# Pairs of projections in one two-bank PSUM tile, in the first halves of a hybrid trunk step

## The chip, the cores and the metric

One core of one Trainium2 chip runs the kernel. The metric is the device time of one execution in microseconds. The engines are PE (TensorE, the matmuls), ACT (ScalarE), DVE (VectorE), POOL (GpSimd) and SP (SyncE, which issues the DMAs). Matmuls write to PSUM, which has eight banks of 2 KB per partition; 512 float32 columns fill one bank. All engines take their instructions in a fixed order that is set when the program is built; they wait for each other through semaphores.

## What is computed

Two layers over 1024 prompt tokens and 8 sample tokens. Each layer projects its input by one wide matrix, sends the parts through three branches (attention in a window of 128, a gated linear recurrence, a Mamba-2 SSD), gates each of them, projects the joined result back and normalises:

```python
def mixer_layer(x, pos, att_cache, lru_conv0, lru_h0, ssd_conv0, ssd_h0, p):
    proj = jnp.einsum('bld,de->ble', x, p['w_in'])
    q, k, v, g_att, x_lru, g_lru, z_ssd, xbc, dt_raw = jnp.split(proj, SPLIT_POINTS, axis=-1)
    q, k = partial_rope(q, pos), partial_rope(k, pos)
    att = swa_prompt(q, k, v, p['att_sinks'])          # swa_sample for the sample tokens
    br_a = att * jax.nn.silu(g_att)
    xl, lru_conv1 = causal_conv(x_lru, lru_conv0, p['lru_conv_w'], p['lru_conv_b'])
    hl, lru_h1 = rglru(xl, lru_h0, ...)
    br_b = hl * jax.nn.silu(g_lru)
    xbc_c = jax.nn.silu(causal_conv(xbc, ssd_conv0, ...))
    dt = jax.nn.softplus(dt_raw + p['ssd_dt_bias'])
    y, ssd_h1 = ssd_scan(xs, dt, a_head, b_ssm, c_ssm, ssd_h0)
    br_c = rms_norm((y + p['ssd_d'] * xs) * jax.nn.silu(z_ssd))
    out = jnp.einsum('ble,ed->bld', concat(br_a, br_b, br_c), p['w_out'])
    return layer_norm(DEEPNORM_ALPHA * x + out, p['ln_g'], p['ln_b'])
```

## The kernel before

The channels lie on the partitions and the tokens along the free dimension. The program walks four stages, layer 0 first half, layer 0 second half, layer 1 first half, layer 1 second half. A first half has W = HALF = 512 token columns, a second half 520 (512 and the 8 samples). In each stage 38 projections of 128 output channels run over the input (`project`, called for K, V, Q0 to Q3, the attention gates GA0 to GA3, the eight SSD blocks of each group, here s00 to s07 and s10 to s17, the recurrence's inputs XL0 to XL5 and its gates GL0 to GL5). `ssd_steps` adds a projection of 24 channels for the step sizes, called "steps" here. Then `out_proj` computes eight blocks of 128 channels, four times over, each time over a quarter of the joined branches.

Numbers are split into a high and a low part. So each product of 128x128 weights takes three matmuls (`mac3`): weights high by input high (L270), high by input low (L271), low by high (L272). A projection has 8 such products: 24 matmuls of 512 columns in a first half, in one bank; 48 of 260 columns in a second half, in two banks. A block of `out_proj` has 12 matmuls of 512 columns in a first half. The weights come in by DMA and are split by ACT (L225) and POOL (L226), two projections ahead.

The PSUM pool `ipp` holds two tiles of two banks, with the tag ip, and every call of `ip_tile` takes the next of them. So the projection that is called as number n waits until the result of number n-2 has been read out, its evacuation. In a first half the second bank of each of the two tiles is not used. Four more banks (`mmp`, tag mm) serve all other matmuls. The evacuation of an SSD or XL block is the pair of ACT instructions at the head of `conv` (L321, L322). That of a gate is ACT's tanh and DVE's product in `gate_silu` (L314, L315). K and Q take one ACT instruction (L716), V one (L762), the steps one (L469). A block of `out_proj` takes a DVE addition (L986).

Between projections, `pump` lets the generators of the attention, the SSD and the recurrence go on: `spawn` hands them over, and each call of `pump` counts down their delays. So the small matmuls of the branches stand between the large ones. The framework then orders the instructions of each engine for good: it simulates the schedule with estimated durations, takes the order in which instructions become ready, and inserts the semaphore waits. For each tile it keeps who last wrote and read it, and the next tile in the same place waits for its last reader.

Of the kernel before, what the change touches and what calls it, by code (L numbers as in the profile page):

```python
# [11 lines left out]
F32 = mybir.dt.float32  # L12
# [5 lines left out]
P = 128  # L18
# [4 lines left out]
HALF = 512  # L23
# [27 lines left out]
def tile_trunk(ctx, tc, outs, x_t, cache_k, cache_v, st_lru_conv, st_ssd_conv, st_ssd_h, w_in, w_dt, w_out,  # L51
# [13 lines left out]
    ipp = ctx.enter_context(tc.tile_pool(name="ipp", bufs=2, space=bass.MemoryType.PSUM))  # L65
    mmp = ctx.enter_context(tc.tile_pool(name="mmp", bufs=4, space=bass.MemoryType.PSUM))

    def ip_tile():
        return ipp.tile([P, 2, 512], F32, tag="ip", name="ip")

    def mm_tile():
        return mmp.tile([P, 512], F32, tag="mm", name="mm")
# [7 lines left out]
    def wtile(shape, tag, bufs=1, dt=F32):  # L80
        return wk.tile(shape, dt, tag=tag, name=tag, bufs=bufs)
# [128 lines left out]
    def pump():  # L210
        for t in list(tasks):
            t[0] -= 1
            if t[0] <= 0:
                try:
                    t[0] = next(t[2])
                except StopIteration:
                    tasks.remove(t)
# [38 lines left out]
    def weights(key):  # L256

        load_weights()
        k, w = loaded.pop(0)
        assert k == key  # L260
        return w
# [7 lines left out]
    def mac3(out, wh, wl, xh, xl, first, last):  # L269
        PE.matmul(out, wh, xh, start=first, stop=False)  # L270
        PE.matmul(out, wh, xl, start=False, stop=False)  # L271
        PE.matmul(out, wl, xh, start=False, stop=last)  # L272
# [7 lines left out]

    def project(l, x, W, block):
        w = weights((l, block))
        ps = ip_tile()
        for c, (k0, k1) in (((0, (0, 4)), (0, (4, 8))) if W == HALF else ((0, (0, 8)), (1, (0, 8)))):
            pump()
            out, cs = pc(ps, W, c)
            for k in range(k0, k1):
                mac3(out, w.h[:, k, :], w.l[:, k, :], x[0][k // 4][:, k % 4, cs], x[1][k // 4][:, k % 4, cs],
                     k == 0, k == 7)
        return ps  # L290

    def chunks(W):

        return [slice(0, W)] if W == HALF else [slice(0, W // 2), slice(W // 2, W)]

    def pc(ps, W, c):

        if W == HALF:
            return ps[:, 0, :], slice(0, W)
        n = W // 2  # L300
        return ps[:, c, :n], slice(c * n, (c + 1) * n)
# [6 lines left out]
    def sv(ap, W):  # L308
        return ap.rearrange("p (c n) -> p c n", c=2)
# [147 lines left out]
    def ssd_steps(st, l, half, x):  # L457

        W = HALF + NS * half
        ps = ip_tile()  # L460
        pump()
        for c in range(len(chunks(W))):
            out, cs = pc(ps, W, c)
            for k in range(8):
                for i in range(2):
                    PE.matmul(out[:24], wdt[:, l, k, :], x[i][k // 4][:, k % 4, cs], start=k + i == 0,
                              stop=k + i == 8)
        dtr = wtile([24, WMAX], "ev", NE)
        S.activation(sv(dtr[:, :W], W), pv(ps, W, 24), AF.Copy)  # L469

        def rest():
            pt = mm_tile()
            for b in range(4):
                PE.matmul(pt[:, b * 12:b * 12 + 12], dtr[:, b * P:(b + 1) * P], sel, start=True, stop=True)
            if half:
                PE.matmul(pt[:NS, 48:60], dtr[:, HALF:W], sel, start=True, stop=True)
            nd = 48 + 12 * half
            dv = wtile([P, 60], "dv")
            if half:
                G.memset(dv[:, 48:60], 0.0)  # L480
            V.tensor_tensor(dv[:, :48].rearrange("p (b e) -> p b e", b=4),
                            pt[:, :48].rearrange("p (b e) -> p b e", b=4),
                            dtb_bc[:, l, None, :].to_broadcast([P, 4, 12]), ALU.add)
            if half:
                V.tensor_tensor(dv[:NS, 48:60], pt[:NS, 48:60], dtb_bc[:NS, l, :], ALU.add)
            dt = st["dt"] = wtile([P, 60], "dt")
            dsc = wtile([P, 4, 60], "dsc")
            softplus(dt[:, :nd], dv[:, :nd], [dsc[:, i, :nd] for i in range(4)], nd)
            da = st["da"] = wtile([P, 60], "da")
            V.tensor_tensor(da[:, :nd].rearrange("p (b e) -> p b e", e=12),  # L490
                            dt[:, :nd].rearrange("p (b e) -> p b e", e=12),
                            a_bc[:, l, None, :].to_broadcast([P, nd // 12, 12]), ALU.mult)
            if half:

                sdt = wtile([NS, 2, 12], "eda")
                V.tensor_copy(sdt[:, 0, :], dt[:NS, 48:60])
                S.activation(sdt[:, 1, :], da[:NS, 48:60], AF.Exp)
                sdd = dp.tile([2, 12, NS], F32, tag="sdd", name="sdd")
                for e in range(2):
                    dma(sdd[e].rearrange("k b -> b k"), sdt.rearrange("b q (t e) -> b (q t) e", e=2)[:, :, e])  # L500
                dcols = st["dcols"] = wtile([P, 2, 6, NS], "dcols")
                for e in range(2):
                    dma(dcols[64 * e:64 * e + 64].rearrange("p a b c -> p (a b c)"),
                        bview(sdd, e * 96, [[0, 64], [1, 96]]))
            yield 7
            pc = mm_tile()
            PE.matmul(pc[:, 0:48], tri, da[:, :48], start=True, stop=True)
            PE.matmul(pc[:, 64:112], ones, da[:, :48], start=True, stop=True)

            nacs = st["nacs"] = wtile([P, 48], "acs")  # L510
            V.tensor_scalar(nacs, pc[:, 0:48], -1.0, None, op0=ALU.mult)
            cd = st["cd"] = wtile([P, 48], "cd")
            S.activation(cd, pc[:, 64:112], AF.Exp)
            dd = st["dd"] = wtile([P, 48], "dd")
            V.tensor_tensor(dd, pc[:, 64:112], nacs, ALU.add)
            S.activation(dd, dd, AF.Exp)
            V.tensor_tensor(dd, dd, dt[:, :48], ALU.mult)
            yield 1
            pa = mm_tile()
            PE.transpose(pa[:48, :P], nacs, ident)  # L520
            acsT = wtile([48, P], "q", NC)
            V.tensor_copy(acsT, pa[:48, :P])
            acsd = st["acsd"] = dp.tile([48, P], F32, tag="acsd", name="acsd")
            dma(acsd, acsT)
            st["steps"] = True

        spawn("ssd", rest())
# [424 lines left out]
    def out_proj(l, half, mixd, load_next, first):  # L952
        W = HALF + NS * half
        n = W // 2
        r = [u_tile() for _ in range(2)]
        for i in range(2):
            dma(r[i][:, :, :W], xd[l, half][512 * i:512 * i + 512, :W].rearrange("(k p) w -> p k w", p=P))
        cur = first
        for gi, (g, _) in enumerate(GROUPS):
            mh, ml = cur  # L960
            if gi < 3:
                drain(*GROUPS[gi + 1][1])
                cur = load_mix(half, mixd, GROUPS[gi + 1][0])
            if gi == 2:
                load_next()


            split_c = l == LAYERS - 1 and half == 1 and gi == 3
            for part in ((slice(HALF // 2, W), slice(0, HALF // 2)) if split_c else (None,)):
                for op in range(4):  # L970
                    w = weights((l, g, op))
                    for oo in range(2):
                        pump()
                        o = 2 * op + oo
                        ps = ip_tile()
                        if part:
                            products = [(ps[:, 0, :part.stop - part.start], part)]
                        else:
                            products = [pc(ps, W, c) for c in range(len(chunks(W)))]
                        for out, cs in products:  # L980
                            for k in range(4):
                                mac3(out, w.h[:, k, oo * P:oo * P + P], w.l[:, k, oo * P:oo * P + P],
                                     mh[:, k, cs], ml[:, k, cs], k == 0, k == 3)
                        ro, po = r[o // 4][:, o % 4, :W], pv(ps, W)
                        ro, po = (ro[:, part], products[0][0]) if part else (sv(ro, W), po)
                        V.scalar_tensor_tensor(ro, ro, ALPHA if gi == 0 else 1.0, po, op0=ALU.mult, op1=ALU.add)  # L986
                if part and part.start:
                    spawn("norm", norm_last(half, r, (2, 3, 4)))
        return r
# [266 lines left out]
```

## Time and profile before

| | us |
|---|---|
| median of 3 runs (lowest, highest) | 1747.94 (1747.93, 1750.72) |
| the profiled execution, its own time | 1744.72 |
| its span in the trace | 1743.0 |
| PE busy in the span | 1601.8 (92%) |
| DVE, ACT, POOL busy | 1177.5, 960.3, 915.4 |
| mean granted clock of PE | 0.963 of full speed |

The profiled execution took 1.7 us more than its span, and 3.2 us less than the median. The stages lie as follows in the trace: projections of layer 0's first half to 304 us, its out_proj to 412, the second half to 866, layer 1's first half to 1178, its out_proj to 1292, the second half to 1743. In the timeline a row is the start, the duration, the engine, the line, the operation, its output and inputs with their shapes, and in brackets the idle time before it with what ended that.

### The profile page before, as it was taken

What the parts mean: (1) busy time and instruction counts of PE and PEld (TensorE: products, weight loads), DVE (VectorE), ACT (ScalarE), POOL (GpSimd) and SP (SyncE); (2) the same over time, 40 slices, a digit from 0 to 9 for tenths busy, and PEclk for the clock granted to TensorE, in tenths of its full rate; (3) what the DMA queues carried; (4) which work ended last, traced back from release to release, by engine and by line L of the source; (5) the groups of instructions that cost most, each with busy time, mean ns of one, the idle gap of its engine ahead of it and who ended that gap; (6) DMA issues with size and microseconds to landing.
All of it is one profiled execution on the core that took longest, in us unless ns stands there. A gap on an engine that the chain in (4) does not pass through costs nothing. (4 is left out here: it accounts for less than half of the span.)

```text
span 1743.0 us, 29885 instructions
## 1 busy us (share of the span) xinstructions
PE 1601.8 (92%) x10696; PEld 1353.7 (78%) x10696; DVE 1177.5 (68%) x2118; ACT 960.3 (55%) x2066; POOL 915.4 (53%) x866
## 2 busy tenths in 40 slices
PE   8999998899889998889998999988998998988996
PEld 6777765578889887779966777656798997977896
DVE  5756578835955877876488565679336659788835
ACT  5655567723455646675155555666345646566724
POOL 4544655445444667644444445553445547786344
PEclk9999999999899989899999999999999999989999
DMA  6322334732232545455323223347433234453733
GB/s 228 98 87 84 100 97 144 238 114 88 82 110 84 157 122 149 128 200 184 104 68 129 77 88 102 92 135 238 148 117 101 84 111 145 122 149 108 238 121 123
DMA packets 147294, 222.00 MB, mean 127 GB/s; under 512 B 17077, under 2 KB 56961, under 8 KB 147097
## 3 DMA queue, kind: packets, MB, share of 16 engines
q1 hardware_dynamic: 144840, 215.90, 39.4%
q10 hardware_dynamic: 2304, 4.20, 0.7%
q8 instruction: 84, 1.38, 0.3%
q14 instruction: 66, 0.53, 0.1%
HBM read 184.04 MB, written 35.43 MB: 126 GB/s over the span
## 5 line engine op out<-in xcount | busy, mean ns | idle before, releaser
L226 POOL TENSOR_TENSOR wl<-wraw,wh 128x512 fp32r<-128x512 f32 x440 | 619.7, 1426 | 609.4 <-ACT wh L225 557.5
L270 PE MATMUL ip<-u,wh 128*128 128x260 f32 (+3 forms) x2592 | 861.9, 333 | 62.2 <-DVE u L986 20.9
L272 PE MATMUL ip<-u,wl 128*128 128x260 f32 (+3 forms) x2592 | 846.5, 327 | 7.3 <-POOL wl L226 7.2
L271 PE MATMUL ip<-u,wh 128*128 128x260 f32 (+3 forms) x2592 | 847.0, 327 | 0.0
L270 PEld LDWEIGHTS ip<-u,wh 128*128 128x128 f32 x2592 | 500.3, 193 | 130.1 <-issue 21.0
L272 PEld LDWEIGHTS ip<-u,wl 128*128 128x128 f32 x2592 | 499.8, 193 | 52.7 <-POOL wl L226 9.1
L271 PEld LDWEIGHTS ip<-u,wh 128*128 128x128 f32 x2592 | 500.7, 193 | 44.8 <-issue 8.5
L225 ACT ACTIVATE wh<-wraw 128x512 fp32r<-128x512 f32 x440 | 256.5, 622 | 314.4 <-PE ip L271 140.9
L986 DVE SCALAR_TENSOR_TENSOR u<-u,ip 128x512 f32<-128x512 f32 (+3 forms) x136 | 89.0, 655 | 150.6 <-PE ip L272 150.6
L329 DVE SCALAR_TENSOR_TENSOR u<-ev,ssd_p,u 128x512 f32<-128x512 f32 x120 | 117.6, 980 | 27.4 <-ACT u L322 22.1
L827 ACT ACTIVATE sp<-sp,mx 128x257 f32<-128x257 f32 (+1 forms) x128 | 62.4, 490 | 75.6 <-DVE mx L823 75.6
L329 DVE SCALAR_TENSOR_TENSOR u<-ev,lru_p,u 128x512 f32<-128x512 f32 x72 | 79.0, 1098 | 19.7 <-ACT u L322 19.4
L614 ACT ACTIVATE acr<-acr,acs 128x128 f32<-128x128 f32 x192 | 63.0, 393 | 44.4 <-POOL acr L611 30.8
L424 PE MATMUL mm<-u,gw 96*32 96x260 f32 (+1 forms) x576 | 62.0, 495 | 23.6 <-DVE hst L633 11.2
L608 POOL TENSOR_TENSOR cq<-cq,u 128x384 f32<-128x384 f32 x56 | 63.5, 1136 | 34.9 <-ACT cq L607 22.0
L233 DVE TENSOR_TENSOR u<-u 128x512 fp32r<-128x512 f32 (+1 forms) x88 | 71.3, 846 | 12.8 <-ACT u L232 12.7
L616 DVE TENSOR_TENSOR acr<-acr,q 128x384 f32<-128x384 f32 x64 | 45.7, 737 | 35.6 <-ACT q L602 27.6
L823 DVE CUSTOM_DVE_ANT_0 sp<-mm,amask,sp 128x256 f32<-128x256 f32 (+1 forms) x128 | 54.7, 463 | 20.2 <-PE mm L820 20.0
L607 ACT ACTIVATE cq<-acr 128x384 f32<-128x384 f32 x56 | 29.1, 522 | 70.7 <-DMA acr<-acsd 66.4
L232 ACT ACTIVATE u<-u 128x512 fp32r<-128x512 f32 (+1 forms) x88 | 51.7, 626 | 26.1 <-DVE sd L564 12.0
L315 DVE SCALAR_TENSOR_TENSOR u<-ev,ip 128x512 f32<-128x512 f32 (+1 forms) x48 | 33.0, 687 | 40.8 <-ACT ev L314 33.6
L424 PEld LDWEIGHTS mm<-u,gw 96*32 96x32 f32 x576 | 17.0, 114 | 50.0 <-issue 19.8
(281 smaller groups left out, 2216.2 us busy)
## 6 DMA issues: line engine op xcount, KB each, us to landing
wraw<-in_w_in_dram SPq DMA_DIRECT2D x304, 256.0 KB
wraw<-in_w_out_dram SPq DMA_DIRECT2D x136, 256.0 KB
acr<-acsd SPq DMA_DIRECT2D x64, 192.0 KB
u<-mixd SPq DMA_DIRECT2D x32, 260.0 KB
u<-mixd SPq DMA_DIRECT2D x32, 256.0 KB
mixd<-u SPq DMA_DIRECT2D x24, 260.0 KB
h<-in_st_ssd_h_dram SPq DMA_DIRECT2D x32, 192.0 KB
mixd<-u SPq DMA_DIRECT2D x24, 256.0 KB
```

The lines of the kernel that those rows point to most:

```text
L225: S.activation(dh, src, AF.Copy)
L226: G.tensor_tensor(dl, src, dh.bitcast(F32), ALU.subtract)
L233: V.tensor_tensor(dl, raw, dh.bitcast(F32), ALU.subtract)
L270: PE.matmul(out, wh, xh, start=first, stop=False)
L271: PE.matmul(out, wh, xl, start=False, stop=False)
L272: PE.matmul(out, wl, xh, start=False, stop=last)
L329: V.scalar_tensor_tensor(out[:, :HALF], raw[:, t:t + HALF], prm[:, wo + t:wo + t + 1], out[:, :HALF], op0=ALU.mult, op1=ALU.add)
L424: PE.matmul(ps[c0:c1, :n], gw[:, gi, k, b0:b0 + c1 - c0], xc[:96, k, cs], start=True, stop=True, skip_group_check=True)
L608: G.tensor_tensor(cq[i], cq[i], zc[:, None, 3, cs].to_broadcast([P, 3, P]), ALU.mult)
L614: S.activation(acr[i][:, e, :], acr[i][:, e, :], AF.Exp, scale=-1.0, bias=nacs[:, eb + 3 * i + e:eb + 3 * i + e + 1])
L827: S.activation(s[:, kv, :nk + 1], s[:, kv, :nk + 1], AF.Exp, scale=-1.0, bias=mx[:, kv:kv + 1], accum_out=den[:, kv:kv + 1])
L986: V.scalar_tensor_tensor(ro, ro, ALPHA if gi == 0 else 1.0, po, op0=ALU.mult, op1=ALU.add)
```

## The change

`ip_tile` is told the width. In a first half, one call takes a new tile of two banks and gives out its bank 0; the call after it gives out bank 1 of the same tile. Any other width takes a whole tile as before. The pairs go by order of call: (K, V), (steps, Q0), (GA0, s00), (s01, Q1), (GA1, s02), (s03, Q2), (GA2, s04), (s05, Q3), (GA3, s06), (s07, s10), and so on through (s17, XL0), (XL1, XL2), (GL0, GL1), (GL2, XL3), (XL4, XL5), (GL3, GL4), (GL5, first block of out_proj), and the blocks of out_proj two by two.

```diff
-    def ip_tile():
-        return ipp.tile([P, 2, 512], F32, tag="ip", name="ip")
+    second = []
+
+    def ip_tile(W):
+
+        if W == HALF and second:
+            return second.pop()
+        second.clear()
+        t = ipp.tile([P, 2, 512], F32, tag="ip", name="ip")
+        if W == HALF:
+            second.append(t[:, 1:2, :])
+            t = t[:, 0:1, :]
+        return t
...
     def project(l, x, W, block):
         w = weights((l, block))
-        ps = ip_tile()
+        ps = ip_tile(W)
...
     def ssd_steps(st, l, half, x):
         W = HALF + NS * half
-        ps = ip_tile()
+        ps = ip_tile(W)
...
                         o = 2 * op + oo
-                        ps = ip_tile()
+                        ps = ip_tile(W)
```

All lines below L79 move down by ten, so that L270 becomes L280. The order of the instructions moves in the first halves alone. A row of the order is the line, the operation, and the tiles that it writes and reads, with their numbers.

The first place is on PE in layer 0, behind GA0. Before, s00 (tile ip_448) follows GA0 (tile ip_375) in the order of the calls:

```order
L271 MATMUL ip_375<-u_117,wh_311 128x512
L272 MATMUL ip_375<-u_115,wl_312 128x512
L270 MATMUL ip_375<-u_115,wh_311 128x512
L271 MATMUL ip_375<-u_117,wh_311 128x512
L272 MATMUL ip_375<-u_115,wl_312 128x512
L270 MATMUL ip_448<-u_114,wh_365 128x512
L271 MATMUL ip_448<-u_116,wh_365 128x512
```

After, the tile ip_373 holds GA0 in bank 0 and s00 (weights wh_363) in bank 1, and ip_498 begins with s01 (weights wh_436):

```order
L280 MATMUL ip_498<-u_114,wh_436 128x512
L281 MATMUL ip_498<-u_116,wh_436 128x512
L282 MATMUL ip_498<-u_114,wl_437 128x512
L280 MATMUL ip_498<-u_115,wh_436 128x512
L281 MATMUL ip_498<-u_117,wh_436 128x512
L280 MATMUL ip_373<-u_114,wh_363 128x512
L281 MATMUL ip_373<-u_116,wh_363 128x512
L282 MATMUL ip_373<-u_114,wl_364 128x512
```

The block s01, which is called behind s00, has moved ahead of it, and s00 starts in the middle of s01, 14 of whose matmuls stand between GA0's last one and s00's first one.

The second place is on PE where the recurrence's projections begin. Before, XL1 (tile ip_2174), whose place is that of s17, follows XL0 (ip_2130) and a small matmul:

```order
L271 MATMUL ip_2130<-u_117,wh_2019 128x512
L272 MATMUL ip_2130<-u_115,wl_2020 128x512
L270 MATMUL ip_2130<-u_115,wh_2019 128x512
L271 MATMUL ip_2130<-u_117,wh_2019 128x512
L272 MATMUL ip_2130<-u_115,wl_2020 128x512
L619 MATMUL mm_2175<-sd_2075,q_2077 128x384
L270 MATMUL ip_2174<-u_114,wh_2120 128x512
L271 MATMUL ip_2174<-u_116,wh_2120 128x512
L272 MATMUL ip_2174<-u_114,wl_2121 128x512
```

After, s16 is bank 1 of ip_1866, and XL1 takes bank 0 of ip_2160, which is that tile's place:

```order
L280 MATMUL ip_1866<-u_115,wh_1856 128x512
L281 MATMUL ip_1866<-u_117,wh_1856 128x512
L282 MATMUL ip_1866<-u_115,wl_1857 128x512
L634 MATMUL mm_2019<-acr_1914,sd_1923 64x128 x2
L634 MATMUL mm_2019<-cq_1933,hst0_112 64x128
L634 MATMUL mm_2019<-cq_1936,hst0_112 64x128
L634 MATMUL mm_2019<-acr_1914,sd_1923 64x128
L634 MATMUL mm_2019<-acr_1915,sd_1923 64x128
L634 MATMUL mm_2019<-cq_1936,hst0_112 64x128 x2
L634 MATMUL mm_2019<-acr_1915,sd_1923 64x128 x2
L280 MATMUL ip_2160<-u_114,wh_2107 128x512
L281 MATMUL ip_2160<-u_116,wh_2107 128x512
```

The last matmuls of s16 now stand directly ahead of XL1, with ten small matmuls of the SSD between them, where a whole projection stood.

## Rows read from the trace of the kernel before

**Rows 1.** The page: PE's busy time; and POOL's weight split as a group.

```profile
PE 1601.8 (92%) x10696; PEld 1353.7 (78%) x10696; DVE 1177.5 (68%) x2118; ACT 960.3 (55%) x2066; POOL 915.4 (53%) x866
L226 POOL TENSOR_TENSOR wl<-wraw,wh 128x512 fp32r<-128x512 f32 x440 | 619.7, 1426 | 609.4 <-ACT wh L225 557.5
```

**Rows 2.** Windows by stage: length, PE, PEld, DVE, ACT, POOL, clock, DMA, GB/s.

```profile
6.00:304.00 298.00, 285.22 (x1474) 213.89 (x1475) 202.07 (x393) 174.30 (x395) 158.77 (x152) 0.98 0.36 117
304.00:412.00 108.00, 98.28 (x418) 74.67 (x417) 65.52 (x81) 46.77 (x75) 45.66 (x33) 0.97 0.51 166
412.00:866.00 454.00, 414.36 (x3413) 384.29 (x3412) 323.20 (x594) 247.04 (x533) 251.75 (x238) 0.95 0.42 129
866.00:1178.00 312.00, 290.58 (x1497) 218.69 (x1496) 217.70 (x364) 176.46 (x390) 155.76 (x149) 0.97 0.32 100
1178.00:1292.00 114.00, 106.90 (x515) 84.68 (x514) 60.91 (x83) 52.20 (x87) 49.38 (x37) 0.99 0.52 167
1292.00:1743.00 451.00, 406.47 (x3389) 377.50 (x3388) 307.12 (x605) 258.63 (x574) 251.08 (x238) 0.95 0.42 131
```

**Rows 3.** PE's waits, 6 to 304, then 866 to 1178: total, times, longest.

```profile
PE ip L270 <- DVE ga L315: 4.4, 2, 4.1
PE ip L270 <- DVE u L315: 2.0, 1, 2.0
...
PE ip L270 <- DVE u L315: 5.7, 1, 5.7
PE ip L270 <- DVE ga L315: 5.6, 3, 2.8
PE ip L270 <- ACT u L322: 3.5, 2, 3.3
```

**Rows 4.** Timeline, layer 0: GA0's last matmul, s00's, GA0's evacuation, the next start.

```profile
36.84 0.40 PE L272 MATMUL ip<-u,wl 128*128 128x512 f32 x1
...
43.62 0.40 PE L272 MATMUL ip<-u,wl 128*128 128x512 f32 x1
...
47.34 0.67 DVE L315 SCALAR_TENSOR_TENSOR ga<-ev,ip 128x512 f32<-128x512 f32 x1
...
48.07 0.71 PE L270 MATMUL ip<-u,wh 128*128 128x512 f32 x1 [4.06 <-DVE ga L315]
```

**Rows 5.** Timeline, layer 0: the end of s11, its evacuation, and small matmuls.

```profile
152.78 0.40 PE L272 MATMUL ip<-u,wl 128*128 128x512 f32 x1
153.02 0.40 PE L270 MATMUL ip<-u,wh 128*128 128x512 f32 x1
...
154.09 0.58 ACT L321 ACTIVATE ev<-ip 128x512 f32<-128x512 f32 x1
...
154.57 0.77 ACT L322 ACTIVATE u<-ip,ssd_p 128x512 f32<-128x512 f32 x1
...
154.50 0.66 PE L848 MATMUL mm<-sp,vtok 128*64 128x128 f32 x8
```

**Rows 6.** Timeline, layer 0: the last matmul of s16 and its evacuation.

```profile
193.03 0.39 PE L272 MATMUL ip<-u,wl 128*128 128x512 f32 x1
...
195.89 0.69 DVE L315 SCALAR_TENSOR_TENSOR u<-ev,ip 128x512 f32<-128x512 f32 x1 [3.03 <-ACT ev L314]
```

**Rows 7.** Timeline, layer 1: the slowest evacuation, of Q1, and GA0's.

```profile
895.34 0.40 PE L272 MATMUL ip<-u,wl 128*128 128x512 f32 x1
...
907.09 0.68 DVE L315 SCALAR_TENSOR_TENSOR ga<-ev,ip 128x512 f32<-128x512 f32 x1
...
919.77 0.39 PE L272 MATMUL ip<-u,wl 128*128 128x512 f32 x1
...
935.17 0.58 ACT L716 ACTIVATE ev<-ip 128x512 f32<-128x512 f32 x1
```

**Rows 8.** Windows behind two idle stretches of PE, columns as in rows 2.

```profile
48.00:52.00 4.00, 3.93 (x10) 3.12 (x11) 3.73 (x10) 2.94 (x6) 2.55 (x2) 0.57 0.06 21
924.00:929.00 5.00, 3.26 (x8) 2.62 (x9) 5.00 (x11) 3.49 (x9) 2.13 (x3) 0.66 0.65 238
```

## The prediction

> **What bounds the kernel now.** I read the page first. PE is busy 92% of the span and no other engine over 68% [rows 1], so PE carries the time, and a change is worth what it adds to PE's idle time or takes from it. The windows by stage then say where the change can act. The order of the built program has the same PE rows in the second halves before and after (454 and 451 us, the third and the sixth row of [rows 2]), so these 905 us should stay. The first halves hold 298 + 108 + 312 + 114 = 832 us, of which PE is busy 285.2 + 98.3 + 290.6 + 106.9 = 781.0 us, so it idles 51 us [rows 2]. All that the change can save lies in these 51 us; what it can cost has no such limit.
>
> The waits of PE then show how much of that comes from places in PSUM. In the two stretches with projections PE stood still at L270 for an evacuation 4.4 + 2.0 us in layer 0 and 5.7 + 5.6 + 3.5 us in layer 1: 21.2 us in nine waits [rows 3]. The other idle time belongs to weights and to the branches' own chains, which the change leaves as they are.
>
> The timeline shows why so few starts wait. Start n needs the evacuation of n-2, and the whole of n-1 lies between: 24 matmuls at 0.24 us from one to the next (the first two of [rows 5]), 5.8 us, with small matmuls besides. I call the PE work between the last matmul of the awaited projection and the start that waits for it the cover. An evacuation, counted from that last matmul to the end of the last reading instruction, took 2.2 us where ACT was at hand (153.18 to 155.34, [rows 5]), 3.2 us for s16 [rows 6], 10.8 us for GA0 (37.24 to 48.01, [rows 4]) and 15.6 us at most (920.16 to 935.75, [rows 7]). Over the 78 of the two stretches I work out a mean of 5.0 and a median of 4.1 us from the timeline, of which these are the quick end and the slow one. A cover of 5.8 us and more hides most of them.
>
> **The change part by part.** The matmuls, evacuations, weight splits and DMAs keep their number and size. What changes is which start waits for what, and so the order on PE.
>
> First, the waits. The change gives four banks, and by its words four projections have a place. In the built program they don't quite. The waits there go by tiles: the second projection of a pair, in bank 1, waits for the count that the evacuation of bank 0 of its own tile sets; the first projection of a tile waits for both evacuations of the tile two before it. So there are still two chains. Only who waits for whom has changed: the second of a pair waits for its partner, which is called directly ahead of it, and the first of the next pair waits for the second one of the pair before the last.
>
> The order answers to that. PE no longer does 0, 1, 2, 3, but 0, 2, 1, 4, 3: it puts a projection of the other tile between two partners where it can. Of the 74 starts of projections and steps in the two stretches that I can compare, 3 had under 4.4 us of PE work as cover before; in the order after, 31 have. Those 31 have 2.0 us in the median; the other 43 have 4.9 to 15.7 us. The two places quoted with the change show it. XL1 comes ten small matmuls behind s16, whose evacuation it needs; eight small ones take 0.66 us [rows 5], so the cover is about 0.8 us against an evacuation of 3.2 us [rows 6]: 2.4 us of wait, where a whole projection hid it before. And s00 has 14 matmuls of s01, 3.4 us, between GA0 and itself, while GA0's evacuation took 10.8 us. Before, 6.8 us of s00's matmuls lay there and PE still idled 4.06 us [rows 4]; half the cover gone makes this wait some 3.4 us longer.
>
> The sum over all starts: where the evacuation is longer than the cover, the rest is a wait. If each evacuation took as long as before, this gives 42 us in the order before and 94 us in the order after. The rough check is 31 starts x (5.0 - 2.0) = 93 us. Now 42 is twice the 21.2 us that PE really waited, since a wait that has held PE up once holds up what comes after it as well. I take the same half for the 52 us more: +26 us. Three of the entries in the opening of layer 1 hang on one and the same chain on DVE (GA0 and Q1 of [rows 7]), and the wait is paid once: -6. Idle PE has a price behind it: after the idle 4.06 us at 44 us the granted clock was 0.57 for 4 us [rows 4, 8], that is half of full speed for most of it, and it was 0.66 for 5 us around the idle 3.3 us at 922 [rows 3, 8]. The first is (1 - 0.57) x 4 = 1.7 us. Two more such stretches: +3. Last, part of the longer wait is taken from waits that PE has anyway in the branches' chains, about 30 of the 51 us; I take -3 for that. Net: +26 - 6 + 3 - 3 = +20 us.
>
> The bounds. If each evacuation ran at its quickest (2.2 us, [rows 5]) whenever PE waits for it, the waits after would come to 11.5 us, against 21.2 now: -10 us. If all 94 us were paid, +73 us. I stand nearer to the half, because it is what the same sum gave in the order before.
>
> Second, out_proj (108 and 114 us, [rows 2]). Its blocks are paired too, and PE swaps them in the same way (1, 0, 2, 3, 5, 4). Each start still has one block of 12 matmuls, 2.9 us, between itself and the block whose addition it awaits: nothing. The other end would be some tenths for each of 64 blocks, up to 10 us, and is inside the range.
>
> Third, the weights. A projection that is moved ahead needs its weights earlier, and POOL's split takes 1.43 us for a half [rows 1], behind ACT's. The weights are still two projections ahead and the swapped one still comes a whole projection after the one before it, 5.8 us: nothing. Were that cover gone, each would cost two splits, 2.9 us. The opening K, V loses the other tile as cover too: V now waits for K's one ACT instruction, about half a microsecond.
>
> A rule that speaks against this reading: a matmul may write one bank while another engine reads a different one. The Trainium skill says so in "PSUM — Partial Sum Buffer", section "Summary: rules for kernel authors", which wants semaphores by bank. By that rule nothing on the chip asks a second projection to wait for its partner, and the waits would vanish as in the second rival below; the built program waits all the same, and no row here can show what the chip would do without.
>
> **The rivals.** *Evacuations catch up* (not slower). While PE stands still it gives ACT and DVE nothing new, and they are busy 58% and 68% of the first stretch [rows 2]; so each awaited evacuation may come near its 2.2 us. It decides where the evacuation outlasts its cover by less than 21.2 / 31 = 0.7 us at each of the 31 short starts. For it: the order was chosen for short waits. Against it: s16, a plain gate, took 3.2 us with 3.03 us of DVE idle, so ACT came late [rows 6], and ACT splits weights and serves the softmax in between. It gives 1744.7 - 10 + 3.2 = 1738 us.
>
> *The change does what it says* (faster): four projections have a place, no start of the first halves waits, and the 21.2 us go, or 1727 us by the median. Against it stand the counts that the second of each pair waits for.
>
> *No difference*: the waits on evacuations only move other idle time, since the chain of the SSD and the recurrence sets the end of each stretch: 1748 us. Against it, PE idles only 12.8 of the 298 us and 21.4 of the 312 us [rows 2], so there is little to be absorbed in.
>
> *The full price*: waits put the evacuations of the next projections no earlier, each start pays its own, +73 us: 1821 us. It decides if ACT and DVE have as long a queue when PE idles as when it doesn't.
>
> **How the numbers follow.** The profiled execution took 1744.7 us, 3.2 below the median. 1744.7 + 20 + 3.2 = 1768 us. The chances: my forecast and its neighbours, slower by some 5 to 55 us, 0.65; the full price 0.10; evacuations catch up 0.14; the change does what it says 0.02; no difference 0.09. A measurement of this kernel can tell about 0.2%, 3.5 us, from no change. So faster 0.16, the same 0.09, slower 0.75. The range for 8 in 10 reaches from just under the catch-up rival, 1736, to 1800, which leaves out the full price, the second rival and the tail of the first. The cases slower than before alone would span 1753 to 1800.
>
> **What would show it.** The waits of PE at L280 on DVE L325 and on ACT L332 and L726 in the first halves' projections should come to some 40 us instead of 21, in many waits of 1 to 3 us. The two stretches of projections should be longer by some 8 to 12 us each, the out_proj stretches by under 2 us, and the second halves unchanged. XL1 should wait for DVE L325 for about 2 us, and s00 of layer 0 for 7 us. I am wrong if these stretches are no longer than before, if the evacuations behind the short starts take 2.2 us, or if the second halves move.

## The result, and the profile after

The changed kernel took 1755.62 us in the median of 11 runs, against 1747.94 us (11 runs) for the kernel before. The ratio is 1.0051, with a 95% interval from 1.0033 to 1.0069: slower by 8.9 us, between 5.8 and 12.1. The forecast was 20 us more than before. The sign held. The size was more than twice what was measured, and the waits that were to show the mechanism moved the other way, as the list of waits below shows.

The page after the change, first PE's busy time, as in [rows 1], and then the windows by stage, as in [rows 2] (length, busy time of PE, PEld, DVE, ACT and POOL, granted clock, DMA share, GB/s):

```profile
PE 1603.3 (91%) x10696; PEld 1352.0 (77%) x10696; DVE 1167.5 (67%) x2118; ACT 960.5 (55%) x2066; POOL 906.3 (52%) x866
```

```profile
6.00:322.00 316.00, 293.83 (x1507) 216.57 (x1507) 202.96 (x399) 177.04 (x400) 157.41 (x154) 0.98 0.35 115
322.00:421.40 99.40, 93.45 (x383) 73.67 (x384) 59.86 (x75) 42.99 (x69) 42.45 (x31) 0.97 0.51 164
421.40:874.00 452.60, 413.73 (x3416) 382.72 (x3416) 324.27 (x594) 246.91 (x533) 252.00 (x238) 0.95 0.42 130
874.00:1186.00 312.00, 291.80 (x1507) 217.65 (x1505) 210.53 (x364) 177.64 (x390) 153.90 (x151) 0.97 0.31 101
1186.00:1288.00 102.00, 95.07 (x411) 74.22 (x412) 57.66 (x80) 47.04 (x75) 42.39 (x31) 0.98 0.53 178
1288.00:1753.90 465.90, 415.45 (x3479) 387.15 (x3477) 311.25 (x607) 263.84 (x587) 255.12 (x242) 0.95 0.41 128
```

The second half of layer 0 is about as long as before (452.6 against 454 us). That of layer 1 took 466.1 us (1287.8 to 1753.9) against 462.0 (1281 to 1743), with the same matmuls in the same order; so of the 10.9 us between the two profiles 4.1 lie there, outside the stages that the change touches. In layer 0 the projections and out_proj together take 415.4 us, against 406 of [rows 2]: 9.4 more. In layer 1, from the first projection to the first matmul of the second half, they took 413.8 us (874 to 1287.8), against 415.0 by the same marks before (866 to 1281). So the first halves together went from 821.0 to 829.2 us. PE is busy 770.0 and 774.0 us in these stretches: half of the 8.2 us that the first halves grew by is idle time, the other half is time in which the same matmuls took longer. How the loss lies between the stages should not be read too closely, since the same stage differed by up to 3 us between the profiles of the kernel before and of one with the same order on PE (e2 below).

PE's waits after (line, what ended them, total, times, longest), of layer 0's first half (6 to 421.4 us), then of layer 1's (874 to 1287.8), as in [rows 3] but with out_proj:

```profile
PE ip L280 <- ACT wh L235: 11.7, 4, 6.5
PE ip L280 <- DVE u L996: 5.4, 2, 2.7
PE ip L282 <- POOL wl L236: 4.3, 4, 2.7
PE ip L280 <- ACT ev L726: 3.7, 2, 3.3
PE ip L280 <- DVE u L325: 2.8, 3, 1.7
...
PE ip L280 <- ACT wh L235: 7.0, 3, 3.1
PE ip L280 <- DVE u L996: 6.7, 4, 2.5
PE ip L282 <- POOL wl L236: 3.9, 3, 2.7
...
PE ip L280 <- DVE u L325: 1.8, 2, 1.7
...
PE ip L280 <- ACT ev L726: 0.2, 1, 0.2
```

Here is the surprise. The waits for evacuations in the projections (L325, L726) came to 8.5 us, where the forecast had about 41 and the kernel before had 21.2 [rows 3]. The waits for weights (L235, L236) came to 26.9 us; before they were 8.4 us in the same stretches, 6.6 of them for the very first weights. So by the list of waits alone, pairs would be good for evacuations, and the weights would have cost it. The experiments show that this reading is wrong.

### The profile page after: what moved, and what is told of

It is laid out like the page before. It is cut to its first block, busy times and chain, and to the rows that moved or that the text cites. A ratio compares the mean times of both kernels' runs of the same rounds, so it can differ in the third digit from the quotient of the medians.

```text
span 1753.9 us, 29893 instructions
## 1 busy us (share of the span) xinstructions
PE 1603.3 (91%) x10696; PEld 1352.0 (77%) x10696; DVE 1167.5 (67%) x2118; ACT 960.5 (55%) x2066; POOL 906.3 (52%) x866
## 5 line engine op out<-in xcount | busy, mean ns | idle before, releaser
L236 POOL TENSOR_TENSOR wl<-wraw,wh 128x512 fp32r<-128x512 f32 x440 | 611.8, 1408 | 629.2 <-ACT wh L235 564.4
L280 PE MATMUL ip<-u,wh 128*128 128x260 f32 (+3 forms) x2592 | 861.5, 332 | 58.5 <-DVE u L996 18.8
L280 PEld LDWEIGHTS ip<-u,wh 128*128 128x128 f32 x2592 | 500.2, 193 | 128.1 <-ACT wh L235 32.4
L235 ACT ACTIVATE wh<-wraw 128x512 fp32r<-128x512 f32 x440 | 257.4, 622 | 377.4 <-PE ip L281 206.7
L339 DVE SCALAR_TENSOR_TENSOR u<-ev,lru_p,u 128x512 f32<-128x512 f32 x72 | 82.0, 1141 | 10.9 <-ACT u L332 10.8
L243 DVE TENSOR_TENSOR u<-u 128x512 fp32r<-128x512 f32 (+1 forms) x88 | 75.3, 887 | 13.3 <-ACT u L242 13.2
L242 ACT ACTIVATE u<-u 128x512 fp32r<-128x512 f32 (+1 forms) x88 | 52.0, 626 | 29.4 <-DMA u<-mixd 7.6
L626 DVE TENSOR_TENSOR acr<-acr,q 128x384 f32<-128x384 f32 x64 | 46.5, 744 | 21.0 <-ACT q L612 13.7
L673 DVE CUSTOM_DVE_ANT_0 sd<-bb,h 128x128 f32<-128x128 f32 x96 | 54.0, 610 | 5.3 <-POOL h L670 5.1
```

Source lines behind the costliest of these rows:

```text
L235: S.activation(dh, src, AF.Copy)
L236: G.tensor_tensor(dl, src, dh.bitcast(F32), ALU.subtract)
L243: V.tensor_tensor(dl, raw, dh.bitcast(F32), ALU.subtract)
L339: V.scalar_tensor_tensor(out[:, :HALF], raw[:, t:t + HALF], prm[:, wo + t:wo + t + 1], out[:, :HALF], op0=ALU.mult, op1=ALU.add)
L673: V.tensor_tensor_reduce(u[:, t, :], bb[:, b % 2, 1, :], h0[:, t, :], 1.0, 0.0, op0=ALU.mult, op1=ALU.add, accum_out=ysum[:, t, b:b + 1])
```

## The experiments

Two theories stood against each other. **Theory W**: the swap on PE makes a projection start straight behind the one whose weight buffer it takes, and the waits for weights are the loss. **Theory E**, that of the prediction: the second projection of a pair waits for its partner's evacuation, which is directly ahead of it in the order of calls, and a wait for weights only stands where that wait would stand. Times below are medians; each ratio is against the kernel before on the same chip, with its 95% interval.

| | us | ratio |
|---|---|---|
| changed kernel | 1755.6 | 1.0051 [1.0033, 1.0069] |
| e1, four tiles of one bank | 1727.3 | 0.987 [0.985, 0.989] |
| e2, n and n+2 share a tile | 1748.5 | 0.9998 [0.998, 1.0015] |
| e3, pairs, half-sized weight tiles | 1751.8 | 1.0019 [1.0002, 1.0035] |
| e4, before, half-sized weight tiles | 1732.1 | 0.9892 [0.9867, 0.9917] |
| e5, four tiles, half-sized weight tiles | 1718.6 | 0.981 [0.9794, 0.9827] |
| e9, before, one weight tile | 1711.0 | 0.9782 [0.9757, 0.9807] |
| e10, pairs, one weight tile | 1732.0 | 0.9914 [0.9889, 0.9939] |
| e13, pairs, weights in PE's order | 1760.2 | 1.0056 [1.004, 1.0072] |
| e15, four tiles, one weight tile | 1691.0 | 0.967 [0.9658, 0.9683] |

### e1 and e2: the same four banks, cut in other ways

In e1 a first half opens a pool of four one-bank tiles, and a second half one of two two-bank tiles.

```diff
+    def open_places(half):
+        if places:
+            places["stack"].close()
+        places["stack"] = ExitStack()
+        places["pool"] = places["stack"].enter_context(
+            tc.tile_pool(name="ipp", bufs=2 if half else 4, space=bass.MemoryType.PSUM))
...
+        if W == HALF:
+            return places["pool"].tile([P, 1, 512], F32, tag="ip", name="ip")
+        return places["pool"].tile([P, 2, 512], F32, tag="ip", name="ip")
```

> In the first halves four tiles of one bank each, from a pool opened for the stage, instead of two tiles of two banks; weight buffers as before. Start n then waits for the evacuation of n-4. Theory W (the changed kernel loses its time to weight buffers: a swapped projection starts straight behind the one whose buffer it takes): PE goes in the order of the calls, waits for weights stay at those of the kernel before (about 14 us in all at L270 and L272), waits for evacuations in the first halves' projections go from 21 us to under 3: 1725 to 1735 us. Theory E (the time goes to the wait of a second projection for its partner's evacuation): the same, since that wait is gone. Rival, other chains set the end: within 4 us of 1748.

It took 1727.3 us, 22.7 less than before. The windows of e1, the projections and out_proj of layer 0, then of layer 1:

```profile
6.00:299.70 293.70, 283.57 (x1474) 212.09 (x1475) 197.17 (x393) 173.51 (x394) 153.78 (x152) 0.99 0.38 119
299.70:399.30 99.60, 96.72 (x419) 72.13 (x417) 64.13 (x82) 47.85 (x77) 46.99 (x33) 1.00 0.56 179
...
854.90:1156.00 301.10, 285.50 (x1481) 214.87 (x1482) 216.41 (x363) 174.50 (x388) 155.45 (x149) 0.98 0.34 101
1156.00:1256.00 100.00, 97.70 (x432) 73.69 (x431) 60.63 (x81) 49.06 (x78) 47.53 (x34) 1.00 0.59 190
```

The first halves shrank from 821.0 to 794.4 us. PE idles 30.9 instead of 51.0 us and is busy 763.5 instead of 770.0, at a granted clock of up to 1.00. No projection there waited for an evacuation. One part of the expectation was wrong: the waits for weights did not stay at 8.4 us but rose to 19.2 (10.1 and 1.3 on L238, 4.4 and 3.4 on L239), and it was faster all the same. PE running further ahead is a likely reason for the rise, but no run shows it. That was the first sign that a wait for weights need not be a loss.

In e2 tiles are shared by n and n+2 instead of n and n+1.

```diff
-        if W == HALF and second:
-            return second.pop()
-        second.clear()
+        if W == HALF and second and second[0] >= 2:
+            second[0] += 1
+            t = second[second[0] - 2]
+            if second[0] == 4:
+                second.clear()
+            return t[:, 1:2, :]
...
```

> In the first halves projections n and n+2 share a tile, one bank each, so that two in a row lie in different tiles. The second one of a tile then waits for the one two calls before it, the first one of a new tile for the one two calls before it too, as in the kernel before. Theories W and E both expect the order and the waits of the kernel before: 1744 to 1752 us. If two banks of a tile were free of each other on the chip and in the program, it would be faster than 1740.

1748.5 us, no difference from before, and its matmuls stand in the same order as those of the kernel before, all 9,668 of them. The four banks are all in use here, two to a tile, and it gains nothing. So what holds a start back in these programs goes by tiles, not by banks, and what the change costs comes from who shares a tile with whom.

### e3 to e8: more room for the weights

e3 (on the changed kernel) and e4 (on the kernel before) cut each weight tile into two of half the size, so that the split can begin when half of a projection is done.

```diff
-            self.h = wp.tile([P, 1024], F32R, tag="wh", name="wh")
-            self.l = wp.tile([P, 1024], F32R, tag="wl", name="wl")
             for i in range(2):
+                h = wp.tile([P, 512], F32R, tag="wh", name="wh", bufs=4)
+                l = wp.tile([P, 512], F32R, tag="wl", name="wl", bufs=4)
...
```

> The changed kernel with each weight tile cut into two tiles of half the size (four places of 512 columns for the high part and four for the low part, the same memory), so that the split of the first half of a projection's weights can start when the first 12 matmuls of the one two before it are done, some 2.9 us sooner. Theory W: the waits for weights (18.8 us on ACT L235 and 15.6 on POOL L236 at the matmuls in the changed kernel, 7.1 and 7.2 before) fall to half of their excess or less, and the time to 1738 to 1748 us. Theory E: the waits for evacuations are what costs, so no difference from the changed kernel, 1752 to 1759.

> The kernel before with the same half-sized weight tiles, for comparison. Both theories: the weights are a whole projection ahead there, so within 5 us of 1748, and what it gains is to be taken off from what the changed kernel gains by the same cut.

The kernel before gained 19 us by the ratio (17 by the medians), the changed kernel about 5 (1.0019 against 1.0051). Both theories missed on e4; what the kernel before gained by the cut, with only 1.8 us of waits for weights beyond the start, is not explained here. Theory W missed on e3 too: its time is outside the range that W gave and lies at the edge of E's. The waits for weights in e3's first halves were 25.6 us (13.6 and 6.6 on ACT, 2.3 and 3.1 on POOL), hardly less, because in each layer one split of GL's weights stood on ACT behind a splitting of inputs (L242) that waited 4.6 us for DVE: the order on ACT, not the room, kept it. So e3 says little on W by itself.

e5 joins e1 and e4.

> Four places of one bank in the first halves together with the half-sized weight tiles. Four places alone gave 1727 (22 us less) and left 19 us of waits for weights in the first halves (8 before); the half-sized tiles alone gave 1732 to the kernel before. Theory W: with four places the next limit is the weights, so the cut of the weights saves again: 1712 to 1722 us. If both save the same idle time, 1723 to 1730.

1718.6 us, in the range of theory W; it is the fastest kernel here that computes everything, 1.9% below the kernel before, and the two gains add up in part (22.7 and 19 became 33).

e6 to e8 make room for a third weight tile by taking one of the ten large tiles of the tag u away (NU = 9), and e7 and e8 then use three weight tiles.

> The changed kernel with nine instead of ten places for the large tiles of the tag u, which makes room for a third weight tile; the control for the next run. Nothing says that the tenth is idle: 1750 to 1775 us.

> The changed kernel with nine u tiles and three weight tiles of each kind instead of two, loaded three projections ahead. Theory W: the swapped projection no longer takes the buffer that the one directly ahead of it on PE is leaving, so the waits for weights in the first halves (26.9 us in the changed kernel, 8.4 before, 6.6 of them at the very start) fall to 7 to 12 us, and the time is 10 to 20 us below the control with nine u tiles. Theory E: the time is that of the control, within 4 us.

> The kernel before with nine u tiles and three weight tiles. Its waits for weights in the first halves are 8.4 us, 6.6 of them at the very start, which no buffer mends, so theory W expects at most 5 us less than with nine u tiles and two weight tiles; the half-sized weight tiles however saved 17 us there, more than those waits, so 5 to 17 us may be had in other ways: 1730 to 1760 us, depending on what the missing u tile costs.

They took 1793.2, 1797.1 and 1787.9 us. The missing u tile costs far more than what was to be measured, and e6 and e8 are outside their ranges. Still, in e7 the only wait for weights among the nine longest waits of the first 330 us is the 6.3 us at the very start, where e6 had 17.6 us, and no time was won by that: against W, though with another bottleneck beside it.

### e9, e10 and e15: no weights to wait for

These three use K's weights for all the projections of a first half and leave out the loads and splits of the other 37, as their expectations say.

```diff
-        w = weights((l, block))
+        if W == HALF and block != B_K:
+            w = held[0]
+        else:
+            w = weights((l, block))
+            held[:] = [w]
...
```

> The kernel before, with the weights of K used for all the projections of a first half: their loads and splits are left out, 37 projections in each of the two first halves. It is the control for the next run. ACT loses 74 splits of 0.62 us in each first half and POOL 74 of 1.43 us, so evacuations come sooner; PE keeps all its matmuls: 1715 to 1745 us.

> The changed kernel with the same left out (one weight tile for all the projections of a first half), so that no projection there waits for its weights. Theory W: pairs without weights to wait for keep only the gain on evacuations (8.5 instead of 21.2 us in the traces), so it is faster than its control by 5 to 15 us. Theory E: the second of each pair still waits for its partner, so it is slower than its control by 5 us or more. Third: within 4 us of the control, if the evacuations are quick in both once ACT has no splits.

> Four places of one bank with one weight tile for all the projections of a first half, as in e9 and e10 (the loads and splits of 37 projections in each first half are left out). Two places gave 1711, pairs 1732. Theory E: without the wait for the partner the loss of the pairs turns into a gain as in e1: 1690 to 1702. Theory W, by which pairs lose through weights alone, has no account of the 21 us; by it four places here are worth what evacuations cost in e9's projections, 9 us: 1700 to 1706. If PE's order and not the partner's wait costs, 1708 or more.

1711.0, 1732.0 and 1691.0 us: without weights, pairs cost 21 us against their control, and four tiles gain 20. Theory W had pairs 5 to 15 us faster than the control, so it falls here. (e9 was a little faster than expected, and e15 lies in the range of E, at its lower end.) The first halves of e9, of e10 and of e15, layer 0 and layer 1 each:

```profile
6.00:396.90 390.90, 375.08 (x1890) 286.01 (x1891) 235.78 (x473) 183.40 (x394) 90.21 (x111) 1.00 0.27 85
851.20:1243.60 392.40, 380.11 (x1913) 290.10 (x1913) 248.08 (x442) 186.63 (x388) 85.76 (x108) 0.98 0.24 77
```

```profile
6.00:405.60 399.60, 382.70 (x1890) 289.15 (x1891) 233.18 (x473) 181.72 (x394) 91.79 (x111) 0.98 0.26 83
860.30:1263.50 403.20, 383.00 (x1912) 290.81 (x1912) 246.66 (x443) 185.40 (x389) 91.18 (x108) 0.98 0.24 75
```

```profile
6.00:386.20 380.20, 374.84 (x1891) 285.35 (x1891) 234.16 (x474) 183.55 (x396) 91.79 (x111) 1.00 0.28 88
843.90:1225.10 381.20, 375.63 (x1910) 285.61 (x1911) 248.28 (x443) 186.59 (x391) 89.01 (x109) 1.00 0.25 79
```

ACT, DVE and PE have the same work in all three. In e10 PE idles 37.1 us against 28.1 in e9 and is busy 10.5 us longer; in e15 it idles 10.9 us. The longer busy time goes with the clock: 1.00 in both layers of e15, 1.00 and 0.98 in e9, 0.98 in both of e10.

The loss of e10 does not stand where theory E looked for it. PE's waits for evacuations of projections, layer 0 and layer 1, in e9 and then in e10:

```profile
PE ip L270 <- DVE u L319: 2.9, 2, 1.7
PE ip L270 <- DVE ga L319: 2.6, 1, 2.6
...
PE ip L270 <- ACT u L326: 3.1, 1, 3.1
PE ip L270 <- DVE u L319: 2.5, 2, 1.3
```

```profile
PE ip L280 <- DVE u L329: 3.4, 1, 3.4
PE ip L280 <- ACT u L336: 0.4, 1, 0.4
...
PE ip L280 <- DVE u L329: 3.3, 1, 3.3
PE ip L280 <- DVE ga L329: 2.3, 1, 2.3
PE ip L280 <- ACT u L336: 0.9, 2, 0.6
PE ip L280 <- ACT ev L730: 0.2, 1, 0.2
```

They come to 11.1 us in e9 and to 10.5 in e10. Of the 9.0 us more of idle time 6.6 stand in front of small matmuls of the branches (L521, L862, L1021), and more than half of what the first halves lose is busy time. So sharing a tile with the neighbour costs 21 us without any weights to wait for, yet hardly any of it is paid as a wait for an evacuation. Whether it comes from the order that the framework builds around these waits was not tested apart.

### e13 and e14: the weights in PE's order

e13 is the changed kernel with its weights loaded in the order in which PE takes them.

```diff
...
+        if half == 0:
+            for i in range(len(queue) - 34, len(queue), 2):
+                queue[i], queue[i + 1] = queue[i + 1], queue[i]
```

> The changed kernel with the weights of the first halves' projections loaded in the order in which PE takes them there (from s00 on, two neighbours of the calls change places: s01 before s00, GA1 before Q1, and so on), so that a swapped projection's weights no longer go into the buffer that the projection directly ahead of it is leaving. Pairs, calls and evacuations stay. Theory W (the weights cost it): the waits for weights in the first halves go from 26.9 to about 10 us and the time falls by 10 to 18 us, to 1738 to 1747. Theory E (the starts that wait for the partner set the pace, and a wait for weights only stands where one for an evacuation would stand): the waits for weights fall, those for evacuations rise, and the time stays within 5 us of the changed kernel, 1751 to 1761.

1760.2 us: no gain. Its waits on PE in the first half of layer 0 (6 to 418 us), then of layer 1 (871 to 1290.2):

```profile
PE ip L279 <- DVE u L995: 10.0, 3, 4.8
PE ip L279 <- ACT wh L235: 6.3, 1, 6.3
PE ip L279 <- DVE u L324: 5.1, 2, 4.6
PE ip L279 <- ACT u L331: 3.9, 4, 1.7
PE ip L279 <- DVE ga L324: 2.2, 1, 2.2
PE ip L279 <- ACT ev L725: 1.6, 3, 0.7
...
PE ip L279 <- DVE u L995: 11.0, 3, 4.8
PE ip L279 <- DVE u L324: 5.0, 2, 4.6
...
PE ip L279 <- ACT u L331: 2.9, 5, 1.2
...
PE ip L279 <- DVE ga L324: 2.5, 1, 2.5
```

With 0.8 us on POOL's part the waits for weights are 7.1 us, nearly all at the very start: the cause that W named is gone, and the time did not fall. In its place the waits for evacuations in the projections rose from 8.5 to 23.2 us (12.8 and 10.4) and those for out_proj's additions from 12.1 to 21.0. One place shows the exchange. In the changed kernel, GA0 ends at 38.12 us, PE waits for s01's weights twice, and s00 starts when GA0's evacuation is over:

```profile
37.72 0.40 PE L282 MATMUL ip<-u,wl 128*128 128x512 f32 x1
...
39.16 0.50 PE L280 MATMUL ip<-u,wh 128*128 128x512 f32 x1 [1.05 <-ACT wh L235]
...
42.60 0.50 PE L282 MATMUL ip<-u,wl 128*128 128x512 f32 x1 [2.71 <-POOL wl L236]
...
46.37 0.68 DVE L325 SCALAR_TENSOR_TENSOR ga<-ev,ip 128x512 f32<-128x512 f32 x1
...
47.10 0.50 PE L280 MATMUL ip<-u,wh 128*128 128x512 f32 x1
```

In e13 the same s01 runs without a stop, and PE then waits for the same evacuation, which ends at the same time:

```profile
46.45 0.68 DVE L324 SCALAR_TENSOR_TENSOR ga<-ev,ip 128x512 f32<-128x512 f32 x1
...
47.19 0.51 PE L279 MATMUL ip<-u,wh 128*128 128x512 f32 x1 [2.23 <-DVE ga L324]
```

3.76 us of waits for weights went, and s00 starts at 47.19 instead of 47.10 us. The list of waits names what came last at each start, not what the next start would wait for when that is gone.

> As the run before, and each weight tile cut in two as in e3. The cut took 17 us from the kernel before and some 5 from the changed one. Theory W: with the order mended the cut saves as much as in the kernel before, 1722 to 1735. Theory E: at most some 6 us below the run before it.

1766.1 us (1.01 [1.0087, 1.0113]): the cut that took 17 us from the kernel before takes nothing from pairs in this order. Theory W is out by a wide margin, and it is slower even than theory E had it.

### e11 and e12: one part of the change alone

> Pairs in projections and steps alone; out_proj takes a whole tile for each block as before. The stretch from the first projection to the end of out_proj grew by 9.7 us in layer 0 and shrank by 1.0 in layer 1 in the traces. Waits at out_proj's starts for DVE's addition went from 15.7 to 12.1 us. Theory W and E: about the time of the changed kernel, plus up to 4 us: 1752 to 1762.

> Pairs in out_proj alone; projections and steps take a whole tile each as before. Each block still has one other block between itself and the addition that it awaits: within 4 us of the kernel before, 1744 to 1752. If out_proj is what gained 3.6 us in the changed kernel, 1744 to 1747.

```diff
-                        ps = ip_tile(W)
+                        ps = ip_tile(0)
```

The line of out_proj stands for e11; e12 has the same edit in `project` and `ssd_steps`. With pairs in the projections alone (out_proj calls `ip_tile(0)`, which takes a whole tile): 1757.6 us, 1.0047 [1.0033, 1.0062], about the changed kernel. With pairs in out_proj alone: 1759.4 us, 1.0072 [1.0045, 1.0098], where no difference was expected. The two don't add up to the changed kernel, which has both and loses no more than each. In e12's profile out_proj took 107.5 and 107.4 us, against 107.8 and 104.0 before, by the same marks (the first start of out_proj to the first one of the second half). In layer 1 this cuts it short, since a block of e12's out_proj stands behind the first matmuls of the second half: to the end of that block it is 113.7 us, some 4 of them the second half's. The rest of its loss, the larger part, lies in stages in which PE's order is that of the kernel before. Why out_proj's pairs cost anything is not settled here.

## Why the prediction was half right

**What bounds the kernel, and where.** PE's time decides; this held. That the second halves stay was not borne out in full: together they took 2.7 us more, that of layer 1 4.1 more, near the 3 us by which stages of the same order differ. One reading was wrong: the 30 us of idle time beyond the 21.2 were put down to weights and to the branches' chains, but 15.7 of them are out_proj's own waits for its additions.

**Who waits for whom.** The dependence held: none of the 38 second projections in the changed kernel's trace starts before its partner's evacuation has ended (s00 at 47.10, after 47.05 us, above). As the account of the short starts it did not hold. Counted by PE's busy time in the trace between the awaited matmul and the start, 27 starts have a cover of under 4.4 us, and 22 of these are the first of a tile, which waits for the second one of the pair before the last, as XL1 does for s16. Most second ones have another projection between themselves and their partner on PE; their cover is 7.8 us in the median. With each projection in a tile of its own (e1, e15) the same banks gain some 20 us, and with the sharing moved two calls apart (e2) nothing changes. But e1 and e15 also give PE the order of the calls back, so they don't tell the wait from the order that is built around it; in e10 the 33 short starts waited for 0.8 us in all. The rival "the change does what it says" was priced at 1727 us; e1, where it does, took 1727.3. Against e1, the pairing as it was made costs about 31 us.

**The price of a short start.** This is the step that failed: "the rough check is 31 starts x (5.0 - 2.0) = 93 us", and the half of it that followed. The term was +26 - 6 = +20 us of waits for evacuations; in the trace these waits fell by 12.7 us, from 21.2 to 8.5. The mean of 5.0 us was taken over all evacuations of the kernel before. In the changed kernel the evacuations that the 31 short starts await took 2.3 us in the mean and 2.1 in the median, worked out from its timeline in the same way; those awaited behind a long cover took 6.8. By the prediction's own list it is wrong if these take 2.2 us, and that is about what they took; the list also has the stretches that are no longer than before, and layer 1's first half is 1.2 us shorter. That the built order puts the awaited ones first on ACT and DVE and lets the others lie fits these two means, but was not tested apart. XL1 is a fair case. Forecast: a cover of 0.8 us, an evacuation of 3.2, a wait of 2.4. In the changed kernel s16's last matmul ends at 210.76, its evacuation at 213.51, and the wait is 1.66 us:

```profile
210.36 0.40 PE L282 MATMUL ip<-u,wl 128*128 128x512 f32 x1
...
212.83 0.68 DVE L325 SCALAR_TENSOR_TENSOR u<-ev,ip 128x512 f32<-128x512 f32 x1
...
213.65 0.47 PE L280 MATMUL ip<-u,wh 128*128 128x512 f32 x1 [1.66 <-DVE u L325]
```

So the rival "evacuations catch up" was right on what the evacuations do, though not on the end of it. At GA0 the forecast 3.4 us more were not lost either: the pair's order had done more of s01 by then, and s00 and s01 were both done within 0.2 us of the time before.

**The weights at nothing.** "The swapped one still comes a whole projection after the one before it" was false, and is the second step that failed. s01 follows GA0 directly and takes GA0's buffer, so its split can begin only when GA0 is done: 18.5 us more of waits. In the trace this is what lifted PE's idle time above that of the kernel before. That the time did not fall when these waits went (e13) is because waits for evacuations and for out_proj's additions took their place. So the loss came out with the forecast sign by a sum that the forecast did not have: the 8.2 us of the first halves are -12.7 for evacuations, +18.5 for weights, -3.6 for out_proj, +2.0 for the rest of the idle time and +4.0 of busy time. That the sign agrees is in part luck.

**The clock.** +3 us was forecast; the same matmuls took 4.0 us longer in the first halves. Behind the 3.3 us of idle time that ended at 72.7 us the clock of the window 74 to 78 was 0.57, as in [rows 8]. But the clock records of the two traces grant half speed for 41.0 us of the first halves after the change and for 37.5 before, so by this estimate some 1.7 of the 4.0 us are clock. The rest is not explained.

**out_proj at nothing.** In the changed kernel its waits fell by 3.6 us, in e13 they were 5.3 above the kernel before, and pairs in out_proj alone cost 12.6 us by the ratio (e12). The up to 10 us that the prediction kept in its range were the honest part of that step.

How the 8.9 us divide between the short starts, the swapped order of the branches' work and the clock is not settled by these runs. That pairs lose against two places, with the weights out of the way, is shown (e10 against e9, e13); that four real places win is shown (e1, e15). By which of the three they lose stays open.

## What to carry to other kernels

A bank is a place only if the tool that inserts the waits sees it as one: give each result a tile of its own, or at least put neighbours in the order of calls into different tiles, which cost nothing here (e2). When a wait is priced with a mean latency, take the latency of those results that are waited for: here it was 2.3 us, against 5.0 over all. And before a wait in the list is blamed, ask what the same start waits for next; a run that removes the named cause alone (e13) tells. The same goes for the rival cause: e10 lost 21 us with hardly a wait more on the list that its theory named.

## What the runs showed of the hardware

With fewer gaps on PE the same matmuls got quicker: e1 and the kernel before have the same matmuls in the first halves, and PE was busy 763.5 against 770.0 us, at a granted clock of 0.98 to 1.00 against 0.97 to 0.99. The clock records grant half speed there for 13.7 us in e1, against 37.5 before. About a fourth of what four places gained there (6.5 of 26.6 us) is busy time that goes with the clock, not idle time.
